# A hybrid mLSTM and attention encoder layer: two output products of the long set turned into seven block products, with their weights prepared in the first stage

## The chip, the cores and the metric

The kernel runs on one core of one Trainium2 chip. The metric is the device time of one execution in microseconds; lower is better. The kernel before takes 2188.54 us, the median of three runs that lie between 2187.59 and 2189.1. One further execution was profiled.

## The reference, cut to what matters

One encoder layer is applied to two sets of tokens with shared weights: a long set (`x_prompt`, 1 x 1024 tokens) and a short set (`x_sample`, 1 x 512 tokens), each token 1024 wide.

```
h    = rms_norm(x, pre_w)
cols = h @ w_in                      # q|k, v, o, z, gates of the mLSTM; q,k,v of the attention; z; two merge gates
y_m  = mlstm_mixer(...) * silu(m_z)                  # (tokens, 1024)
y_a  = dilated_attention(...) * silu(a_z)            # (tokens, 512)
p_m  = y_m @ w_proj_m                                # 1024 x 1024 weights
p_a  = y_a @ w_proj_a                                #  512 x 1024 weights
merged = sigmoid(g_m) * p_m + sigmoid(g_a) * p_a
out  = merged @ w_out                                # 1024 x 1024 weights
y    = x + rms_norm(out, post_w)
```

The change concerns the last five lines for the long set. Everything is float32 in the reference.

## The kernel before, in words

**How a product is made.** TensorE multiplies in a reduced format, so each float32 operand is split into a high part and a low part (`hi` on ScalarE by a copy, `lo = x - hi` on VectorE), and one product of a 128x128 block of weights with 128x512 activations takes three matmuls of 128x512: hi·hi, lo·hi, hi·lo. These three are one *step* (`mm3`, lines 230 to 236). A product over 1024 inputs sums eight steps in one PSUM bank; then VectorE evicts it.

**The stages**, by the time in the profiled execution:

- 0 to 231 us: input norm and value products of the long set.
- 231 to 955 us: 38 "pair iterations" (`unit_pair`). Each loads the weights of two 128-column units (`pw_raw`), lets GpSimd (POOL) form sums of them (`psum_w`), splits raw weights and sums into high and low (`phla`, `phlb`, line 764 is the low part), and does the 1024x1024 product for 1024 tokens as seven block products instead of eight (84 matmuls, 19 us). What follows the products differs: 12 attention iterations, then four times (conv, conv, gate), then 8 "zo" and 2 "az".
- 955 to 1776 us: the mLSTM of the long set, the attention of the long set, and the mLSTM of the short set with the mix of the long set's three attention groups. Between their matmuls TensorE takes *fill*: a list of dense units for the short set (its w_in product and others), one step at a time, taken from a generator (class `Fill`).
- 1776 to 2026 us: attention of the short set ("attention B", 48 rounds), with fill between its small matmuls.
- 2026 to 2096 us: "combine B" mixes the three attention groups of the short set, four 128-token tiles t = 0 to 3: weights of the groups (lines 2033 to 2043), three scaled copies (L2050), two adds (L2056), four transposes on TensorE into `tp` (L2061), a product with the gate (L2063). Fill runs between them.
- 2096 to 2178 us: the rest of the fill, alone.

**The fill of the late stages.** From step 768 on (`SHORT`) the fill is: 32 steps left of the short set's units; for each 512-token half of the long set w_proj_m (64 steps), w_proj_a (32) and w_out (64); the same 160 for the short set; 512 steps in all. `branches` makes w_proj_m and w_proj_a, `final` w_out. Each unit's 512 KB of weights is loaded raw into `wraw` by the POOL queue and split by `split_w` (L296 on ScalarE, L302 on VectorE). `STEPS = (316, 260, 192, 290, 86)` gives the number of steps for five stages: 290 over the 48 rounds of attention B, 86 over combine B. The remaining 136 run alone.

**What sets the order.** Engines run their instructions in program order. That order comes from the generators above: a round or a combine part asks the fill for its share of steps, and the splits, evictions and DMA issues belonging to a step are emitted with it. In the late stages the POOL queue issues the loads (`N.side`), SP the stores.

## Time and profile before

| | |
|---|---|
| median of three runs | 2188.54 us (2187.59 to 2189.1) |
| span of the profiled execution | 2185.1 us |
| last TensorE instruction ends | 2177.8 us |
| busy: TensorE / VectorE / ScalarE / GpSimd | 2173.5 / 1460.8 / 1085.1 / 704.2 us |
| moved by DMA | 395.62 MB, mean 181 GB/s |

The profiled execution's own time is its span, 2185.1 us. A busy time counts the union of the instructions' windows. Matmuls are pipelined and their ends are modelled, so the mean duration of a matmul is longer than the distance from one start to the next; the rate is read from starts. In the rows of the groups the columns are line, engine, operation, output<-inputs, shapes and count, then busy time, mean ns of one, then the engine's idle time before them and what ended it. In the windows, `(x222)` is the number of instructions in the stretch.

### The profile page before, as it was taken

How to read it: one execution, taken by the hardware profiler on the slowest of the kernel's cores; microseconds unless marked ns; L12 is line 12 of the kernel's file. 1: busy time of each engine (PE TensorE's matmuls, PEld its weight loads, DVE VectorE, ACT ScalarE, POOL GpSimd, SP SyncE). 2: the span in 40 equal slices, each digit the busy share in tenths (PEclk: the TensorE clock that was granted, in tenths of full speed). 3: DMA queues.
4: the chain of work that ended last, by engine and by line, in shares of the span. 5: the costliest groups of instructions: out<-in, count | busy, mean ns of one | idle time of the engine just before them, and what ended most of it. 6: DMA issues, size and time to landing. Idle time of an engine off the chain costs nothing.

```text
span 2185.1 us, 33611 instructions
## 1 busy us (share of the span) xinstructions
PE 2173.5 (99%) x11626; PEld 1857.3 (85%) x11626; DVE 1460.8 (67%) x2927; ACT 1085.1 (50%) x2228; POOL 704.2 (32%) x989
## 2 busy tenths in 40 slices
PE   9999999999999999999999999999999999999998
PEld 8988888888888888888888889999788888888887
DVE  8766564657778555547888775574668855656674
ACT  7322333444444343446777656666756544554332
POOL 1000332333333222326776650011045522232331
PEclk9999999999999999999999999999999999999999
DMA  3642454733333222367646558877668786776772
GB/s 139 193 139 73 146 162 144 227 110 116 107 115 114 75 82 97 135 216 261 202 164 225 175 167 262 240 241 196 203 233 278 248 288 205 229 261 187 242 240 106
DMA packets 205748, 395.62 MB, mean 181 GB/s; under 512 B 36393, under 2 KB 117993, under 8 KB 205578
## 3 DMA queue, kind: packets, MB, share of 16 engines
q1 hardware_dynamic: 175272, 281.39, 40.2%
q0 software_dynamic: 26704, 99.50, 13.8%
q10 hardware_dynamic: 3602, 12.59, 1.4%
q8 instruction: 92, 1.51, 0.3%
q14 instruction: 78, 0.64, 0.1%
HBM read 274.71 MB, written 118.69 MB: 180 GB/s over the span
## 4 chain that ended last, share of the span: by engine, by line
PE 97%; DVE 1%; ACT 1%; DMA 1%; issue 0%; POOL 0%; DVEq 0%; POOLq 0%; ACTq 0%
PE d L233 14%; PE d L235 14%; PE d L234 14%; PE dense L233 13%; PE dense L234 13%; PE dense L235 13%; PE lg L1801 2%; PE pt L1831 2%; PE o L1874 1%; PE num L233 1%; PE num L235 1%; PE num L234 1%; PE num L1494 1%; PE o L1853 1%; PE a L1201 1%; PE kv L233 1%
## 5 line engine op out<-in xcount | busy, mean ns | idle before, releaser
L233 PE MATMUL dense<-H,wh 128*128 128x512 f32 x664 | 269.3, 406 | 0.0
L234 PE MATMUL dense<-H,wh 128*128 128x512 f32 x664 | 260.3, 392 | 0.0
L235 PE MATMUL dense<-H,wl 128*128 128x512 f32 x664 | 260.2, 392 | 0.0
L233 PE MATMUL d<-Hh,phla 128*128 128x512 f32 x608 | 236.5, 389 | 0.0
L235 PE MATMUL d<-Hh,phla 128*128 128x512 f32 x608 | 236.5, 389 | 0.0
L234 PE MATMUL d<-Hl,phla 128*128 128x512 f32 x608 | 236.5, 389 | 0.0
L302 DVE TENSOR_TENSOR wl<-wraw,wh 128x1024 fp32r<-128x1024 f32 (+1 forms) x121 | 150.8, 1248 | 57.9 <-ACT wh L296 57.8
L235 PE MATMUL d<-Hh,phlb 128*128 128x512 f32 x456 | 177.4, 389 | 0.0
L233 PE MATMUL d<-Hh,phlb 128*128 128x512 f32 x456 | 177.4, 389 | 0.0
L234 PE MATMUL d<-Hl,phlb 128*128 128x512 f32 x456 | 177.4, 389 | 0.0
L296 ACT ACTIVATE wh<-wraw 128x1024 fp32r<-128x1024 f32 (+1 forms) x124 | 128.1, 1036 | 62.1 <-PE dense L234 24.3
L235 PEld LDWEIGHTS dense<-H,wl 128*128 128x128 f32 x664 | 124.7, 188 | 28.1
L782 POOL TENSOR_TENSOR psum_w<-pw_raw 128x512 f32<-128x512 f32 x38 | 56.7, 1492 | 271.1 <-DMA pw_raw<-w_in 259.9
L1820 DVE CUSTOM_DVE_ANT_0 ls<-lg,bias 128x256 f32<-128x256 f32 (+2 forms) x240 | 78.7, 350 | 90.3 <-PE lg L1801 61.7
L233 PEld LDWEIGHTS dense<-H,wh 128*128 128x128 f32 x664 | 125.0, 188 | 16.4 <-issue 1.2
L234 PEld LDWEIGHTS dense<-H,wh 128*128 128x128 f32 x664 | 125.2, 189 | 14.7
L235 PEld LDWEIGHTS d<-Hh,phla 128*128 128x128 f32 x608 | 114.1, 188 | 23.7
L234 PEld LDWEIGHTS d<-Hl,phla 128*128 128x128 f32 x608 | 114.1, 188 | 23.7
L233 PEld LDWEIGHTS d<-Hh,phla 128*128 128x128 f32 x608 | 114.1, 188 | 23.7
L800 POOL TENSOR_TENSOR psum_w<-pw_raw,psum_w 128x512 f32<-128x512 f32 x38 | 49.3, 1298 | 254.2 <-DVE phla L764 254.2
L1824 ACT ACTIVATE ls<-ls,nm 128x256 f32<-128x256 f32 (+1 forms) x192 | 87.3, 456 | 70.2 <-DVE nm L1822 47.0
L233 PE MATMUL d<-v,Hh 128*128 128x484 f32 (+1 forms) x336 | 121.3, 361 | 0.1
(665 smaller groups left out, 5838.8 us busy)
## 6 DMA issues: line engine op xcount, KB each, us to landing
pw_raw<-w_in SPq DMA_DIRECT2D x76, 512.0 KB, 3.9
wraw<-w_in SPq DMA_DIRECT2D x63, 512.0 KB, 4.4
aqk_a<-pwk SPq DMA_DIRECT2D x32, 512.0 KB, 6.7
wraw<-w_pm POOLq DMA_DIRECT2D x24, 512.0 KB, 5.9
wraw<-w_out POOLq DMA_DIRECT2D x24, 512.0 KB, 3.7
Q<-aqk_a SPq DMA_DIRECT2D x20, 512.0 KB, 6.3
wraw<-w_v POOLq DMA_DIRECT2D x22, 430.0 KB, 6.5
aqk_b<-sw SPq DMA_DIRECT2D x36, 256.0 KB, 7.2
```

The costliest lines, as they stand in the source:

```text
L233: nc.tensor.matmul(out, lh, rh, start=start, stop=False, **kw)
L234: nc.tensor.matmul(out, lh, rl, start=False, stop=False, **kw)
L235: nc.tensor.matmul(out, ll, rh, start=False, stop=stop, **kw)
L296: high = nc.scalar.activation(hi[:, :n], raw[:, :n], AF.Copy)
L302: low = (self.lows or nc.vector).tensor_sub(lo[:, :n], raw[:, :n], hi[:, :n].bitcast(F32))
L782: self.nc.gpsimd.tensor_add(s[:, 0], ws[1][:, 0], ws[1][:, 1])
L800: nc.gpsimd.tensor_sub(s[:, 1], wa[:, 1], s[:, 1])
L1201: nc.tensor.matmul(p[:, c - c0], kT[:, ct, c * P:(c + 1) * P], qT[:, ct, c * P:(c + 1) * P], start=ct == 0, stop=ct == 1)
L1801: nc.tensor.matmul(lg[:, hh], q[hh][:, qs], z.rearrange("p (n j) -> p n j", j=P)[:, pair], start=z is k[hh], stop=z is not k[hh])
L1820: nc.vector.tensor_tensor_reduce(out=ls[rows, hh], in0=ts["lg"][hh][rows, of], in1=bt[rows, hh, by], scale=1.0, scalar=NEG, op0=OP.add, op ...
L1824: self.held = self.held[-3:] + [nc.scalar.activation(ls[:, hh], ls[:, hh], AF.Exp, bias=nm[:, hh:hh + 1], accum_out=ot[:, 128 + hh:129 + hh])]
L1831: nc.tensor.transpose(pp[:, hh * nk + x], ts["ls"][:, hh, x * P:(x + 1) * P], self.ident)
```

## The change

For the long set, w_proj_m and w_out become seven block products over all 1024 tokens at once. Inputs, weights and outputs are cut into 2 x 2 blocks of 512; three of the seven products use a raw quadrant of the weights (0, 1 and 3 in `QUADS`), four a sum of quadrants (4 to 7); the sums of activations are made on VectorE in the late stage (`outputs`: `combined`, `third`, `second`), split there, and multiplied. Per product 16 steps, seven products: 112 steps for w_proj_m and 112 for w_out, where there were 128 and 128. After step 768 the fill has 32 + 112 + 64 + 112 + 160 = 480 steps.

The weights of these products, and w_proj_a, are now split in the first stage. Each of the first 32 pair iterations takes one extra job: 16 `pre_plain` (load 512 KB raw, split it) and then 16 `pre_sums` (load 1 MB, two or four additions on POOL, split), each with a store of 1 MB of high and low parts to a DRAM scratch `pre`. In the late stage `load_pre` loads these parts ready made (1 MB a unit) in place of load and split. The short set's w_proj_m and w_out are still loaded raw and split late; its w_proj_a comes from `pre`.

The long set's input is copied to its output by eight DRAM to DRAM copies early in the program; in the late stage 16 DMAs of the POOL queue add the normalised result onto it (`accum_op`), so its `xo` loads and plain stores are gone. `STEPS` becomes `(316, 260, 192, (6, 5), 16, 50)`: six steps a round for the first 32 rounds of attention B, five for the last 16 (272), then 16 and 50 in combine B; 142 steps remain after it.

```diff
-STEPS = (316, 260, 192, 290, 86)
+STEPS = (316, 260, 192, (6, 5), 16, 50)
+QUADS = (0, 1, 5, 6, 3, 4, 7)
+PRE_A, PRE = 28, 32
...
+    def pre_split(self, x, units, sb, to):
+        nc, n = self.nc, x.shape[1]
+        hl = sb.tile([P, 2, 2, BLK], F32R, name="phlb", bufs=2)
+        nc.scalar.activation(hl[:, 0, :n], x, AF.Copy)
+        nc.vector.tensor_sub(hl[:, 1, :n], x, hl[:, 0, :n].bitcast(F32))
+        for j, u in enumerate(units):
+            y = hl.rearrange("p z a c -> p z (a c)") if to is None else hl[:, :, j]
+            dst = self.pre[u] if to is None else self.pre[u, :, :, to]
+            nc.sync.dma_start(dst.rearrange("z p c -> p z c"), y.bitcast(F32))
...
+    def pre_sums(self, i, sb):
+        nc, q = self.nc, self.a["w_q"]
+        u, c, both = i // 4, slice(i // 2 % 2 * BLK, (i // 2 % 2 + 1) * BLK), i % 2
+        ws = []
+        for b in range(2):
+            w = sb.tile([P, 2, BLK], F32, name="pw_raw", bufs=4)
+            nc.sync.dma_start(w, q[2 * b:2 * b + 2, u, :, c].rearrange("q p c -> p q c"))
+            ws.append(w)
+        wa, wb = ws
+        s = sb.tile([P, 2, BLK], F32, name="psum_w", bufs=2)
+        nc.gpsimd.tensor_add(s[:, 0], wb[:, 0], wb[:, 1])
+        nc.gpsimd.tensor_sub(s[:, 1], s[:, 0], wa[:, 0])
+        if both:
+            nc.gpsimd.tensor_sub(s[:, 1], wa[:, 1], s[:, 1])
+            nc.gpsimd.tensor_sub(s[:, 0], wa[:, 0], wb[:, 0])
+        self.pre_split(s, [4 * QUADS.index(j) + u for j in ((6, 7) if both else (4, 5))], sb, c)
...
+    def load_pre(self, u):
+        hi, lo = self.wsplit.pop(0)
+        self.wsplit.append((hi, lo))
+        for z, x in enumerate((hi, lo)):
+            self.loaded = self.side.dma_start(x[:, :1024].bitcast(F32), self.pre[u, z])
+        return hi[:, :1024], lo[:, :1024]
...
+    def outputs(self, T, before):
...
+        def final(weights):
...
+            def close(b, t, ys):
...
+                for h, y in enumerate(ys):
+                    nc.vector.scalar_tensor_tensor(y, y, s[:, 6:7], pw[:, c], op0=OP.mult, op1=OP.mult)
+                    self.adds.append((n + 5 + 4 * h, lambda y=y, c=c: nc.gpsimd.dma_start(T.y[r0:r0 + P, c], y, accum_op=OP.add)))
...
-            units += N.branches(A, 1, 1, finals[:1]) + N.branches(B, 0, 0, finals[1:2]) + finals[2:]
+            first, final = N.outputs(A, short[-4:])
+            units = short[:-4] + first + N.branches(B, 0, 0, [final]) + [last]
...
+                        if early:
+                            job, *x = early.pop(0)
+                            job(*x, sb)
+                        if kind == "conv":
+                            with tc.issue_after(N.split_end.ins):
+                                t = rows.pop(0)
+                                nc.sync.dma_start(A.y[P * t:P * (t + 1)], A.x[P * t:P * (t + 1)])
```

In combine B the order on TensorE around the first transpose of the mix (`tp`, from the operand `X`) was, before:

```order
L233 MATMUL dense<-Q_17486,H_18682 128x512
L234 MATMUL dense<-Q_17486,H_18682 128x512
L235 MATMUL dense<-Q_17486,H_18683 128x512
L2061 MATMUL tp_20301<-ident,X_20055 128x128 x4
L233 MATMUL dense<-Q_17486,H_18682 128x512
L234 MATMUL dense<-Q_17486,H_18682 128x512
L235 MATMUL dense<-Q_17486,H_18683 128x512
```

and is now (`sw`, `V0b`, `V1b`, `wh_7463` belong to the last block product of the long set's w_out; `H_20408` and `X_20409` are high and low of the short set's y_m):

```order
L235 MATMUL dense<-wh_7463,V1b 128x512
L236 MATMUL dense<-wl_7464,V1b 128x512
L237 MATMUL dense<-wh_7463,V1b 128x512
L235 MATMUL dense<-H_20408,wh_7465 128x512
L236 MATMUL dense<-X_20409,wh_7465 128x512
L237 MATMUL dense<-H_20408,wl_7466 128x512
L2110 MATMUL tp_20629<-ident,X_20364 128x128 x4
L235 MATMUL dense<-H_20408,wh_7465 128x512
L236 MATMUL dense<-X_20409,wh_7465 128x512
```

The first transpose moved from the middle of the long set's last w_out to three matmuls behind its end, in the short set's w_proj_m. Between the four transposes there were 42, 45 and 42 dense matmuls; there are now 33, 30 and 33.

On VectorE the stretch around the product with the first `tp` (L2063 before, L2112 now) was:

```order
L2050 TENSOR_TENSOR Q_20056<-V1a,cw_20231 128x512 x3
L302 TENSOR_TENSOR wl_7153<-wraw_7147,wh_7152 128x1024
L2266 SCALAR_TENSOR_TENSOR ss<-ss 128x1
L2268 TENSOR_TENSOR mg<-dense,postw 128x512
L2056 TENSOR_TENSOR Q_20056<-Q_20056 128x512
L2271 SCALAR_TENSOR_TENSOR xo_17492<-sw_7265,ss,xo_17492 128x512
L2271 SCALAR_TENSOR_TENSOR xo_17493<-mg,ss,xo_17493 128x512
L302 TENSOR_TENSOR wl_7149<-wraw_7146,wh_7148 128x1024
L2063 TENSOR_TENSOR az_20052<-tp_20301,az_20052 128x512
L2056 TENSOR_TENSOR Q_20056<-Q_20056 128x512
```

and is now (L2105 the last add that the first transpose reads, L2446 and L2471 the end of the long set's w_out, L2198 the low parts of the short set's y_m, L304 the low parts of its raw weights):

```order
L2105 TENSOR_TENSOR X_20364<-X_20364 128x512
L2446 SCALAR_TENSOR_TENSOR H_19733<-H_19733,ss,postw 128x512
L2446 SCALAR_TENSOR_TENSOR H_20136<-H_20136,ss,postw 128x512
L2198 TENSOR_TENSOR K_20411<-ymr_17801,H_20410 128x512
L2084 TENSOR_TENSOR cw_20553<-V1a,cw_20553 128x24
L304 TENSOR_TENSOR sw<-wraw_7459,sw 128x1024
L2446 SCALAR_TENSOR_TENSOR H_19733<-H_19733,ss,postw 128x512
L2446 SCALAR_TENSOR_TENSOR H_20136<-H_20136,ss,postw 128x512
L2471 TENSOR_TENSOR H_19733<-H_19733,dense 128x512
L2441 SCALAR_TENSOR_TENSOR ss<-ss 128x1
L2112 TENSOR_TENSOR az_20361<-tp_20629,az_20361 128x512
L304 TENSOR_TENSOR wl_7464<-wraw_7460,wh_7463 128x1024
```

Before, the second add of the second mix stood directly behind the product with the first `tp`; now 24 instructions stand between that product and the add that the second transpose waits for.

In the pair iterations the SP queue held only the pair's loads and the iteration's stores:

```order
L777 DMA pw_raw<-w_in 128x1024 x2
L243 DMA qk_a<-pwk 128x1024 x2
L777 DMA pw_raw<-w_in 128x1024 x4
L243 DMA qk_a<-pwk 128x1024 x2
L777 DMA pw_raw<-w_in 128x1024 x2
```

and now has the job's loads (`w_q`) and stores (`pre`) between the two loads of a pair:

```order
L815 DMA pw_raw<-w_q 128x2x512 x2
L245 DMA qk_a<-pwk 128x1024 x2
L779 DMA pw_raw<-w_in 128x1024
L799 DMA pre<-phlb 128x2x512 x2
L779 DMA pw_raw<-w_in 128x1024
```

The pair's second load now stands behind a store that waits for the job's split on VectorE.

324 lines of the change are left out of this document (301 added, 23 removed).

## The prediction

> **What bounds the kernel now.** I read the totals first, then the chain of waits, TensorE's waits, the windows by stage, and the timeline of one stretch. The page:
>
> ```profile
> span 2185.1 us, 33611 instructions
> PE 2173.5 (99%) x11626; PEld 1857.3 (85%) x11626; DVE 1460.8 (67%) x2927; ACT 1085.1 (50%) x2228; POOL 704.2 (32%) x989
> PEclk9999999999999999999999999999999999999999
> PE 97%; DVE 1%; ACT 1%; DMA 1%; issue 0%; POOL 0%; DVEq 0%; POOLq 0%; ACTq 0%
> ```
>
> TensorE is busy from end to end at a full granted clock, and the chain that ended last is 97% TensorE. Its waits, all four of them:
>
> ```profile
> PE d L2370 <- DMA Hh<-prew: 2.3, 1, 2.3
> PE d L476 <- ACT Hh L470: 0.5, 1, 0.5
> PE d L420 <- DVE u2b L417: 0.5, 1, 0.5
> PE d L235 <- DVE Hl L472: 0.4, 1, 0.4
> ```
>
> Together 3.7 us in the whole run. So a matmul removed comes off the time, and everything else costs nothing until it makes TensorE wait. The question is which engine has little room where the change adds work. Windows (columns: stretch, length, then busy time and instructions of PE, PEld, DVE, ACT, POOL, then clock, DMA share, GB/s):
>
> ```profile
> 400.00:450.00 50.00, 50.00 (x222) 41.42 (x221) 32.45 (x32) 23.68 (x20) 19.16 (x14) 1.00 0.71 211
> 592.90:611.90 19.00, 19.00 (x86) 15.73 (x85) 16.95 (x17) 8.93 (x9) 7.27 (x6) 1.00 0.29 104
> 630.90:650.00 19.10, 19.10 (x86) 15.79 (x85) 11.63 (x13) 6.54 (x7) 7.06 (x9) 1.00 0.36 116
> 1776.00:1800.00 24.00, 24.00 (x132) 20.75 (x131) 14.20 (x37) 14.71 (x34) 6.29 (x12) 1.00 0.90 316
> 1850.00:1900.00 50.00, 50.00 (x278) 43.39 (x278) 34.99 (x90) 26.99 (x72) 14.51 (x27) 1.00 0.72 236
> 2050.00:2096.00 46.00, 45.87 (x209) 37.71 (x208) 39.54 (x83) 12.79 (x22) 19.05 (x33) 1.00 0.85 283
> ```
>
> Two places stand out on VectorE: a conv pair iteration (592.9 to 611.9, 16.95 of 19 us busy) and combine B (39.54 of 46). A gate iteration (630.9 to 650) has room, and so has attention B (1850 to 1900).
>
> **What is removed from TensorE.** Two products of 128 steps become 112 each: 32 steps in all, and by the lists of instructions the matmuls of 128x512 fall by 96. Their price is the distance between starts, not the duration shown:
>
> ```profile
> 2065.20 0.39 PE L234 MATMUL dense<-Q,H 128*128 128x512 f32 x1
> 2065.43 0.39 PE L235 MATMUL dense<-Q,H 128*128 128x512 f32 x1
> 2065.66 0.60 PE L2061 MATMUL tp<-ident,X 128*128 128x128 f32 x4
> 2066.01 0.48 PE L233 MATMUL dense<-Q,H 128*128 128x512 f32 x1
> 2075.67 0.60 PE L2061 MATMUL tp<-ident,Q 128*128 128x128 f32 x4
> ```
>
> 42 dense matmuls and one transpose group (0.35 us from its start to the next) take 2075.67 - 2065.66 = 10.01 us, so 0.23 each; where no transpose lies near, the distance is 0.225 to 0.227 (the first window: 222 in 50 us). 96 x 0.227 = **21.8 us saved**. (By the 0.39 of the rows it would be 37.)
>
> **Combine B.** In both kernels the four transposes need operands that VectorE mixes. Before, they are 42 to 45 dense matmuls apart (10 us); after, 30 to 33 (7.0 to 7.8 us), and the first comes 3 matmuls behind the end of the long set's w_out, on whose results VectorE has just then a pile of work. What VectorE's instructions cost is again the distance from start to start:
>
> ```profile
> 2059.56 0.18 DVE L2039 TENSOR_TENSOR wd<-wd 128x8 f32<-128x8 f32 x1
> 2059.78 0.17 DVE L2040 TENSOR_TENSOR wd<-wd 128x8 f32<-128x8 f32 x1
> 2061.64 1.89 DVE L2050 TENSOR_TENSOR Q<-V1a,cw 128x512 f32<-128x512 f32 x3
> 2063.45 1.22 DVE L302 TENSOR_TENSOR wl<-wraw,wh 128x1024 fp32r<-128x1024 f32 x1
> 2064.58 0.15 DVE L2266 SCALAR_TENSOR_TENSOR ss<-ss 128x1 f32<-128x1 f32 x1
> 2064.65 0.69 DVE L2268 TENSOR_TENSOR mg<-dense,postw 128x512 f32<-128x512 f32 x1
> 2065.25 0.69 DVE L2056 TENSOR_TENSOR Q<-Q 128x512 f32<-128x512 f32 x1
> 2065.85 0.75 DVE L2271 SCALAR_TENSOR_TENSOR xo<-sw,ss,xo 128x512 f32<-128x512 f32 x1
> 2066.51 0.75 DVE L2271 SCALAR_TENSOR_TENSOR xo<-mg,ss,xo 128x512 f32<-128x512 f32 x1
> ```
>
> A split of 128x1024 holds the engine 1.13 us, a 128x512 0.60, with a scalar operand 0.66, a small dependent one about 0.2 (0.07 where independent). The rows' durations run past the next start. The Trainium skill, "Perfetto Trace Analysis", section "Optimizing Scalar/DVE Operations", says that a shown latency counts an overhead about twice because the write acknowledgement overlaps the next instruction; the trace agrees (0.69 shown, 0.60 from start to start). By full durations the sum below would come out some 3 us larger (38 large ones by 0.07 to 0.09).
>
> I anchor at the TensorE matmul that ends the last tile of product 5 of the long set's w_out. From there to the second transpose TensorE has 84 dense matmuls and one transpose group: 84 x 0.227 + 0.35 = 19.4 us. In VectorE's order, from the eviction of that tile to the add that the second transpose reads, stand: 5 splits of the short set's raw w_proj_m (5 x 1.13 = 5.65), 6 evictions (3.6), 8 normalising products (8 x 0.66 = 5.3), 7 splits of y_m rows (4.2), 6 scaled copies and 4 adds of the mixes (6.0), the gate product with the first transpose (0.6), one eviction of the short set (0.66), 24 small ones (4.8). Sum 30.8 us. The difference, **11.4 us, is a wait of TensorE**, most of it at the second transpose. About half is forced even if VectorE were on time at the last eviction of w_out: behind it stand 13.8 us of work, and TensorE has 36 matmuls and a transpose group there, 8.5 us. This gives the lower bound of 5.3; less than that needs VectorE faster than in any row. The upper bound: what VectorE itself waits for comes on top. The rows of ScalarE and DMA that bear on it:
>
> ```profile
> 2073.00 1.22 DVE L302 TENSOR_TENSOR X<-wraw,X 128x1024 fp32r<-128x1024 f32 x1 [1.33 <-ACT X L296]
> ...
> L296 ACT ACTIVATE wh<-wraw 128x1024 fp32r<-128x1024 f32 (+1 forms) x124 | 128.1, 1036 | 62.1 <-PE dense L234 24.3
> wraw<-w_pm POOLq DMA_DIRECT2D x8, 512.0 KB, 6.3
> Q<-az_b POOLq DMA_DIRECT2D x1, 256.0 KB, 8.8
> ```
>
> The fifth raw w_proj_m is loaded when the third split frees its buffer; issue about 0.5, landing 6.3, the high part 1.04 make 7.9 us, and VectorE has 8.4 us of other work up to the split. It fits with 0.5 to spare; a landing of 8.8, the longest row of this stage, would add 2. Waits for ScalarE like the 1.33 us of the first row are possible too. So 5.3 to 17, and I take 11.4, the sum without them. After the second transpose VectorE has 4 to 10 us of work for each 7 us of matmuls, and nothing more is late; the wait costs the stage's end one for one.
>
> **The pair iterations.** Each of the first 32 gets a load, a high part on ScalarE, a low part on VectorE (1.13) and a store; 16 have 2 or 4 additions on POOL. TensorE's order there is unchanged. ScalarE is busy 9 of 19 us and DMA at 0.29 to 0.36: 1.5 to 2 MB more per 19 us is some 80 to 105 GB/s beside 104 to 116, below the 316 seen. That is hidden. The stores stand on SP ahead of a load of the next pair; the load is wanted a third of an iteration later, with the splits due only at the second and fourth product. VectorE's room is the issue, since additions on POOL stretch its two-input work:
>
> ```profile
> 583.58 2.20 DVE L764 TENSOR_TENSOR phla<-pw_raw,phla 128x1024 fp32r<-128x1024 f32 x1
> 584.65 2.28 POOL L785 TENSOR_TENSOR pw_raw<-pw_raw 128x512 f32<-128x512 f32 x1
> L764 DVE TENSOR_TENSOR phla<-psum_w,phla 128x1024 fp32r<-128x1024 f32 x6 | 7.3, 1218 | 0.0
> L782 POOL TENSOR_TENSOR psum_w<-pw_raw 128x512 f32<-128x512 f32 x5 | 6.9, 1382 | 31.8 <-DMA pw_raw<-w_in 31.8
> ```
>
> The same split takes 2.20 beside an addition and 1.22 alone: one addition can cost VectorE 1 us. A conv iteration with a job then needs 16.95 + 1.13 + 2 to 4 = 20.1 to 22.1 us of 19.04, a gate iteration 11.63 + 1.13 + 2 to 4 = 14.8 to 16.8. Two convs (one with 2, one with 4 additions) overrun by 4.1; the gate gives 2.3 to 4.3 back, and the splits have about 5 us of slack (due at the fourth product, three products of 2.7 us into the iteration, less the split). Of four triples the first has mostly plain jobs. So the loss is between 0 and 9.2 (if no gate gave anything back: 1.04 + 1.04 + 3.04 + 3.04 + 1.04); I take 1.0, near the low end, because the triple's sum, 57, just fits 57.1. The Trainium skill, "Perfetto Trace Analysis", same section, says that GpSimd and VectorE share a read port and that moving work from one to the other might not help: the stretched pair of rows agrees, and it speaks against summing here.
>
> **Attention B.** Gone: late splits of the long set's weights. New: 96 more VectorE instructions of 128x512 (58 us) against 12 fewer of 128x1024 (13.6), so 44 us more in 250. VectorE is busy 28 to 35 of 50 us there and would be at 0.75 to 0.88. Single rounds are heavier, and a late high and low part delays one step; attention's own small chains cover it with other steps only in part. 0 to 5 us (one round is 5.2), taken as 0.5. DMA: a unit is 1 MB instead of 512 KB, one for every eight steps, that is for some 7 us at six steps a round of 5.2 us, so 512 KB more make 75 GB/s; on 316 in the densest window that is 391, but there the fill is still the old 32 steps, and on the 236 of the later window it is 311. Hidden, with four units loaded ahead. The x to y copies lie on SP in front of the value stores, in a stretch in which DMA does nothing:
>
> ```profile
> 20.00:50.00 30.00, 29.36 (x203) 27.44 (x202) 29.13 (x41) 22.82 (x46) 1.08 (x1) 1.00 0.00 1
> ```
>
> POOL's new 16 adding DMAs replace 16 loads and 16 stores.
>
> **Sum.** -21.8 + 11.4 + 1.0 + 0.5 = -8.9 us. The span would be 2176.2; the profiled execution stands 3.4 us below the median, so the forecast in runs is 2188.5 - 8.9 = **2179.6 us**.
>
> **Rivals.** (1) *All hidden.* The four PSUM banks and matmuls still in hand let VectorE catch up, no wait at the transposes: -21.8, 2166.7. For it: the present combine B is at 39.54 of 46 busy and TensorE waits 0.13. Against: the order puts both evictions and mixes in one queue. Chance 0.13. (2) *VectorE overruns in the conv iterations and gates don't give back*: 9.2 in place of 1.0, so -0.7, 2187.8; against it the gate's 11.63. With milder forms, 0.21 for a result within 0.2% (4.4 us, about what can be told from no change). (3) *Slower: the fifth w_proj_m weights come late.* Everything up to the second transpose stands behind their split on VectorE, one for one. Landing must exceed 6.3 by 0.5 + 8.9 = 9.4 us, 15.7 us in all, before the gain is gone; the adding DMAs queue ahead of that load on POOL, each of them waiting for a normalising product. At 20 us: +4.3, 2192.8, and each later raw unit then drags too, 2195. Chance with other losses 0.14. (4) That the matmuls don't fall is excluded by the lists of both kernels.
>
> **Numbers.** The main case (a gain of 4.4 to 18) has 0.52, all hidden 0.13, so faster 0.65; same 0.21; slower 0.14. The range runs from all hidden, 2166, to 2191, into rivals 2 and 3 but not to their ends.
>
> **What would show it.** 6490 matmuls of 128x512 on TensorE; a wait of TensorE for VectorE of 8 to 14 us at the line of the transposes (now L2110), split between first and second, with VectorE busy without a gap there; none or 1 to 2 us before 955 us at conv iterations; attention B shorter by some 18 steps. No wait at the transposes, or waits for DMA there, would make the sum wrong; so would a conv iteration longer than 19.04 us three times in a row.

## The result and the profile after

The changed kernel is slower: 2224.62 us, median of four runs (2223.09 to 2226.32), against 2188.82 for the kernel before on the same chip (2187.59 to 2189.78). The ratio is 1.0165, with a 95% interval of 1.0151 to 1.018. The forecast was 2179.6, with a range from 2166 to 2191. The page of the profiled execution, whose span is 2224.6 us (before 2185.1):

```profile
span 2224.6 us, 33846 instructions
...
PE 2171.1 (98%) x11530; PEld 1847.5 (83%) x11530; DVE 1549.0 (70%) x3011; ACT 1084.2 (49%) x2248; POOL 810.4 (36%) x1053
...
PEclk9999999999999999999999999999999999999899
...
DMA packets 233655, 469.05 MB, mean 211 GB/s; under 512 B 38249, under 2 KB 120361, under 8 KB 233354
```

TensorE has 96 instructions fewer, as forecast, but is busy only 2.4 us less; VectorE has 88 us and GpSimd 106 us more work; 73 MB more are moved. TensorE's longest waits, which before were four of together 3.7 us:

```profile
PE d L237 <- DVE phla L766: 12.3, 7, 2.1
PE tp L2110 <- DVE cw L2092: 5.9, 1, 5.9
PE tp L2110 <- DVE X L2105: 5.4, 1, 5.4
PE lg L1847 <- DVE ot L1866: 4.0, 1, 4.0
PE dense L235 <- DVE H L2471: 3.1, 1, 3.1
```

Three places wait: `d` (products of the pair iterations, for the low parts of their weights), `lg` (first logits of attention B) and the transposes `tp` with their surroundings in combine B. Windows that begin and end at the same TensorE instructions show how much each place lost (columns as above: length, then busy time and count of PE, PEld, DVE, ACT, POOL, then clock, DMA share, GB/s). First the kernel before:

```profile
573.80:707.10 133.30, 133.30 (x590) 110.36 (x589) 102.49 (x103) 55.23 (x57) 48.57 (x43) 1.00 0.32 112
...
1772.30:1809.70 37.40, 37.40 (x203) 32.29 (x202) 22.77 (x59) 22.11 (x53) 11.40 (x22) 1.00 0.92 320
1809.70:2018.00 208.30, 208.30 (x1152) 177.09 (x1150) 125.80 (x341) 102.08 (x280) 55.70 (x103) 1.00 0.68 217
2018.00:2177.80 159.80, 159.59 (x726) 130.87 (x721) 101.17 (x188) 53.28 (x100) 46.89 (x85) 1.00 0.60 202
```

and the changed kernel: pair iterations 18 to 24 (counted from 0), the start of attention B, the rest of it, and combine B to the end.

```profile
575.00:729.70 154.70, 141.00 (x589) 112.99 (x588) 127.06 (x114) 60.58 (x66) 85.61 (x65) 0.97 0.57 196
...
1799.20:1844.50 45.30, 40.30 (x204) 33.93 (x203) 20.51 (x60) 17.24 (x47) 8.76 (x17) 0.92 0.86 304
1844.50:2043.80 199.30, 197.73 (x1101) 167.43 (x1099) 130.66 (x370) 82.85 (x264) 52.57 (x100) 1.00 0.77 245
2043.80:2216.00 172.20, 155.54 (x680) 125.72 (x675) 104.84 (x205) 50.27 (x105) 56.89 (x91) 0.96 0.68 206
```

In the first row the same matmuls take 154.7 us instead of 133.3. Of the 21.4 us, 13.7 are idle time (154.70 - 141.00); the other 7.7 are shown as *busy* time, at a mean clock of 0.97. The whole ledger, from starts of the same TensorE instructions in both traces (a matmul less counts 0.227 us):

| stage | before | changed | matmuls fewer | loss |
|---|---|---|---|---|
| up to the first pair product | 231.0 | 232.3 | | 1.3 |
| pair iterations | 723.4 | 744.7 | | 21.3 |
| mLSTM and attention of the long set, mLSTM of the short | 817.9 | 822.2 | | 4.3 |
| attention B, to its 31st `lg` | 37.4 | 45.3 | | 7.9 |
| attention B, the rest | 208.3 | 199.3 | 51: 11.6 | 2.6 |
| combine B to the last TensorE instruction | 159.8 | 172.2 | 45: 10.2 | 22.6 |
| behind it | 7.3 | 8.6 | | 1.3 |
| span | 2185.1 | 2224.6 | 21.8 | 61.3 |

So the 21.8 us are there, and 61.3 us were lost elsewhere: 61.3 - 21.8 = 39.5. How far one trace can be trusted for a stage is seen in the experiments below, where an edit leaves a stage as it is: the pair iterations then take 743.5 to 745.1 us, the start of attention B 44.4 to 46.4, its rest 198.4 to 199.3, combine B 170.8 to 173.7. The first row takes 231.0 to 232.4 and the third 819.2 to 822.8, so their 1.3 and 4.3 us are one trace's figures.

**Clock.** TensorE's timeline behind one wait of the pair iterations:

```profile
580.27 0.39 PE L236 MATMUL d<-Hl,phla 128*128 128x512 f32 x1
582.49 0.50 PE L237 MATMUL d<-Hh,phla 128*128 128x512 f32 x1 [1.82 <-DVE phla L766]
...
583.58 0.63 PE L237 MATMUL d<-Hh,phla 128*128 128x512 f32 x1
584.00 0.63 PE L235 MATMUL d<-Hh,phla 128*128 128x512 f32 x1
...
586.47 0.40 PE L235 MATMUL d<-Hh,phla 128*128 128x512 f32 x1
```

Behind a wait of 1.82 us the matmuls start 0.42 to 0.43 us apart for some 3 us, then 0.23 again: seven of them, 1.4 us on top of the wait. Of six waits of 1.8 to 2.1 us in this stage three had such a tail and three had none. In all, 22 matmuls of the row start 0.41 to 0.43 us apart, which makes 4.4 of the 7.7 us. The other 3.3 are not in such tails: the first distance behind a wait is 0.34 us, and idle time is counted only from the modelled end of the matmul ahead, 0.39 us behind its start, so that each wait is shown some 0.16 us too short. The Trainium skill, "TensorE: Matmul & The Clock Gate", Part 1, describes a clock that falls to half behind an idle window of about 3.4 us and gives 426.7 ns from start to start at half rate for this width, with windows that run free of the kernel. The 0.427 us and the length of the tail agree; that waits of about 2 us are enough, some of the time, is what this trace adds.

**VectorE in a conv iteration with a sum job** (the timeline of the changed kernel ahead of the first late product):

```profile
561.64 1.94 DVE L766 TENSOR_TENSOR phlb<-pw_raw,phlb 128x1024 fp32r<-128x1024 f32 x1
563.51 4.55 DVE L878 SCALAR_TENSOR_TENSOR pwk<-c,cws,pwk 128x1024 f32<-128x1024 f32 x2
567.98 1.78 DVE L766 TENSOR_TENSOR phlb<-psum_w,phlb 128x512 fp32r<-128x512 f32 x1
...
575.29 2.29 DVE L766 TENSOR_TENSOR phla<-pw_raw,phla 128x1024 fp32r<-128x1024 f32 x1
```

and GpSimd in the same microseconds, with the job's additions:

```profile
562.58 2.15 POOL L820 TENSOR_TENSOR psum_w<-psum_w,pw_raw 128x512 f32<-128x512 f32 x1
...
566.94 2.27 POOL L823 TENSOR_TENSOR psum_w<-pw_raw 128x512 f32<-128x512 f32 x1
```

A split of 128x1024 takes 1.94 us beside the job's additions instead of 1.22, and 2.29 beside the pair's own additions that follow them. The last row (`phla`) ends at 577.58, and the matmul that reads it starts at 577.63. From 554.8 to 585.4 VectorE has no idle time of more than 0.11 us. How much room was used up is seen at the low part for the second product of iteration 18. In the kernel before, it is ready 3.77 us early:

```profile
572.00 1.22 DVE L764 TENSOR_TENSOR phla<-psum_w,phla 128x1024 fp32r<-128x1024 f32 x1
...
576.99 0.39 PE L235 MATMUL d<-Hh,phla 128*128 128x512 f32 x1
```

Over iterations 14 to 25 this lead is 3.8 to 6.0 us before. In the changed kernel it is 2.3 us in iteration 15, 1.0 in iteration 17 and gone (0.05) in 18, 20, 21, 23 and 24. At 19, 22 and 25 it is 1.0 to 2.0 us again, and that is about what TensorE itself was slowed by half rate just before (some 1.75).

**Combine B.** VectorE's timeline around the last eviction of product 5 (first row: its wait for the groups' sums; then the first and the last instruction of the pile that the prediction summed):

```profile
2079.14 0.17 DVE L2082 TENSOR_TENSOR cw<-V0a 128x8 f32<-128x8 f32 x1 [9.26 <-DMA V0a<-og_b]
...
2081.37 0.68 DVE L2470 TENSOR_TENSOR H<-H,dense 128x512 f32<-128x512 f32 x1
...
2110.19 0.69 DVE L2105 TENSOR_TENSOR Q<-Q 128x512 f32<-128x512 f32 x1
```

From 2081.37 to 2110.88 it is 29.5 us, with 0.91 us idle in it; the prediction's sum was 30.8. TensorE's two waits at the transposes are 5.9 and 5.4, together 11.3 us, as forecast (8 to 14). But the 9.26 us ahead of VectorE's pile were not in the prediction, nor TensorE's wait of 3.1 us for an eviction that stands on VectorE behind that wait. The DMA issues of that stretch (size, median us to landing), in the kernel before

```profile
V0a<-og_b SPq DMA_DIRECT2D x1, 792.0 KB, 4.0
...
og_b<-sg SPq DMA_DIRECT2D x2, 132.0 KB, 2.4
```

and in the changed one:

```profile
V0a<-og_b SPq DMA_DIRECT2D x1, 792.0 KB, 7.1
...
y_prompt<-K POOLq DMA_DIRECT2D x3, 256.0 KB, 8.8
...
og_b<-sg SPq DMA_DIRECT2D x2, 132.0 KB, 10.0
```

The store of the last attention sums took 10 us instead of 2.4. The load of the mix reads what it wrote, so SP stood until it landed, and the load was itself slower.

### The profile page after: what moved, and what is told of

Its sections match the earlier page's. It is cut to its first block, busy times and chain, and to the rows that moved or that the text cites. A ratio compares the mean times of both kernels' runs of the same rounds, so it can differ in the third digit from the quotient of the medians.

```text
span 2224.6 us, 33846 instructions
## 1 busy us (share of the span) xinstructions
PE 2171.1 (98%) x11530; PEld 1847.5 (83%) x11530; DVE 1549.0 (70%) x3011; ACT 1084.2 (49%) x2248; POOL 810.4 (36%) x1053
## 4 chain that ended last, share of the span: by engine, by line
PE 59%; DVE 6%; DMA 4%; issue 4%; ACT 1%; POOL 1%; SPq 0%; DVEq 0%; POOLq 0%; ACTq 0%
PE dense L235 11%; PE dense L236 11%; PE dense L237 11%; PE d L237 4%; PE d L235 4%; PE d L236 4%; PE lg L1847 2%; DVE pwk L878 2%; PE pt L1877 2%; PE o L1920 1%; PE num L235 1%; PE num L236 1%; PE num L237 1%; DVE phla L766 1%; PE num L1540 1%
## 5 line engine op out<-in xcount | busy, mean ns | idle before, releaser
L237 PE MATMUL dense<-H,wl 128*128 128x512 f32 x688 | 271.4, 395 | 0.0
L237 PE MATMUL d<-Hh,phla 128*128 128x512 f32 x608 | 239.4, 394 | 12.3 <-DVE phla L766 12.3
L235 PE MATMUL d<-Hh,phla 128*128 128x512 f32 x608 | 238.5, 392 | 1.4 <-ACT phla L765 1.4
L237 PEld LDWEIGHTS dense<-H,wl 128*128 128x128 f32 x688 | 130.3, 189 | 29.3
L304 DVE TENSOR_TENSOR wl<-wraw,wh 128x1024 fp32r<-128x1024 f32 (+1 forms) x96 | 120.8, 1260 | 29.7 <-ACT wh L298 29.7
L298 ACT ACTIVATE wh<-wraw 128x1024 fp32r<-128x1024 f32 (+1 forms) x99 | 101.7, 1030 | 47.8 <-PE dense L236 20.0
L237 PE MATMUL d<-v,Hl 128*128 128x484 f32 (+1 forms) x336 | 120.6, 359 | 0.4 <-DVE Hl L474 0.4
```

Source lines behind the costliest of these rows:

```text
L235: nc.tensor.matmul(out, lh, rh, start=start, stop=False, **kw)
L237: nc.tensor.matmul(out, ll, rh, start=False, stop=stop, **kw)
L298: high = nc.scalar.activation(hi[:, :n], raw[:, :n], AF.Copy)
L304: low = (self.lows or nc.vector).tensor_sub(lo[:, :n], raw[:, :n], hi[:, :n].bitcast(F32))
```

## Experiments on the pair iterations

Each edit is against the changed kernel; "stage" is the time from the first to the last product of the pair iterations, 723.4 us before and 744.7 in the changed kernel. The letters of the theories change between the expectations: the store of a job, which holds a `phlb` buffer that the pair needs, is rival B in the first run and theory C in the later ones, where B is the second raw tile.

**Additions left out.**

```diff
-        nc.gpsimd.tensor_add(s[:, 0], wb[:, 0], wb[:, 1])
-        ... (all of the job's additions)
+        s = wa
```

> The 16 sum jobs of the pair iterations split the raw quadrants as loaded; their 2 or 4 additions on GpSimd are left out (so four of the seven weight blocks hold other values). Loads, splits and stores stay. Measured before this run: the pair iterations cost 21.4 us more than in the kernel before, 13.7 of them waits of TensorE, the rest matmuls at a lower clock behind the waits. Theory A, VectorE is overrun because the additions on GpSimd stretch its two-input work: a conv iteration then needs some 18.2 of 19.04 us, the waits go to 0 to 2 us, the stage loses 3 us or less, and the time is about 2204. Rival B, the job's store holds the phlb buffer that the pair's own split needs (ScalarE waits 36 us for such stores between 540 and 760 us): the loss stays at 15 us or more, the time at 2218 to 2224.

2219.8 us (2215.28 to 2220.73), ratio 1.0138 [1.0123, 1.0153]; stage 741.6. Still 18.2 of the 21.3 us are lost, in iterations 18, 21, 23 and 24 (the changed kernel loses in 20 too), though the additions are gone from GpSimd; this is what rival B had forecast. So the additions are not a necessary cause.

**One raw tile instead of two, additions kept.**

```diff
-        wa, wb = ws
+            break                # after the first load
+        wa = wb = ws[0]
```

> A sum job loads one raw tile (512 KB) in place of two and adds the halves of that tile; number and size of additions, low parts and stores stay as they are. The values of the sums are wrong. Theory A (additions and VectorE's room): the pair stage still loses 17 to 21 us, 2220 to 2225. Theory B (the second raw tile): the loss falls to 0 to 5 us, 2203 to 2209. Theory C (stores): still 17 to 21.

2224.86 us (2223.63 to 2225.38), ratio 1.0164 [1.0149, 1.0179]; stage 743.8. Nothing gained: the second load is not a necessary cause either.

**Both left out** (both edits above).

> A sum job loads one raw tile and splits it without any addition: sum jobs become plain jobs in load, split and store (32 alike; values of the sums wrong). With both loads and no additions the pair stage lost some 17 us. Theory B: the loss falls to 0 to 3 us, 2203 to 2207. Theory C: it stays at 14 to 17 us, 2216 to 2221. Theory A holds that the additions were half of it and VectorE's room the rest: 3 to 10 us, 2206 to 2214.

2209.47 us (2208.96 to 2209.85), ratio 1.0094 [1.0079, 1.0109]; stage 730.0, loss 6.6. TensorE's wait for `phla` in the kernel with additions and one tile:

```profile
PE d L237 <- DVE phla L766: 12.1, 10, 2.1
```

and in this one, with a wait of ScalarE beside it:

```profile
PE d L237 <- DVE phla L766: 1.8, 5, 0.5
```

```profile
ACT phlb L765 <- DMA pre<-phlb: 97.8, 30, 7.0
```

So *either* part of a sum job, additions or second raw tile, is enough to lose 18 to 20 us, and a job with neither loses 6.6. ScalarE's total wait for stores to free `phlb` does not tell these kernels apart: it is 97.8 us here, where little was lost, and 90.8 in the changed kernel. Which product of TensorE waits does tell them apart. In the changed kernel and in the one with one tile it is always the first or second product of an iteration, for `phla`, at the end of VectorE's work (or of ScalarE's behind it). In the kernel without additions more than half of the wait is at the last product, for `phlb`:

```profile
PE d L235 <- ACT phlb L765: 5.8, 4, 2.5
PE d L237 <- DVE phla L766: 5.5, 6, 1.4
PE d L237 <- DVE phlb L766: 1.2, 3, 0.5
```

There the high part that ScalarE makes for this product starts at 595.02, 658.34 and 722.46 us in iterations 18, 21 and 24, each time 0.10 or 0.11 us behind the landing of a job's store (594.92, 658.23 and 722.36): the store holds the buffer. It was issued 10.0 to 11.8 us into these iterations; with one tile and no additions it was issued at 6.6 to 8.2, and the product gets its operand with hardly a wait. So two chains are seen, each enough alone: VectorE's work where there are additions, a job's late store where there are two tiles and no additions.

**Jobs in other iterations, same work.** In the changed kernel the sum jobs begin in iteration 16 and the loss in iteration 18; the three conv iterations with plain jobs (12, 13, 15) took 19.04 us, like all attention ones. So the list was re-ordered: plain jobs into the eight convs, sums into four attention iterations, the gates and zo.

```diff
+                    plain, added = early[:16], early[16:]
+                    early = plain[:8] + added[:4]
+                    for i in range(4):
+                        early += plain[8 + 2 * i:10 + 2 * i] + [added[4 + i]]
+                    early += added[8:]
```

> Only the list of jobs is re-ordered: the 16 plain jobs now lie in the first 8 attention iterations and in the 8 conv iterations, the 16 sum jobs in the last 4 attention iterations, the 4 gate and the 8 zo ones. Same work in total. In the changed kernel the pair stage loses 21.4 us, all of it in iterations 18 to 24 (convs and their gates with sum jobs). Theory A (VectorE and GpSimd together have no room in a conv iteration for a sum job: additions, their stretching of VectorE and the low part): the loss goes to 0 to 4 us, the kernel takes 2203 to 2209. Theory B (a sum job takes two of the four raw-weight buffers and delays the pair's own weights, whatever the iteration): the loss moves to the attention and zo iterations, 10 to 20 us remain, 2214 to 2224. Theory C (the store of a job holds a buffer of high and low parts, plain jobs too): the convs still lose, 2218 to 2224.

2207.9 us (2206.55 to 2210.5), ratio 1.0089 [1.0074, 1.0104]; stage 730.3, loss 6.9. No work was taken away and 14.4 of 21.3 us are gone; the attention, gate and zo iterations carry the sum jobs in 19.04 us each, but for 2.2 us in the first zo. The wait for `phla` is 4.7 us (six times). Theory B (the second raw tile, wherever it stands) is out, and C (the stores) as the main cause of the 21.3. Theory A's forecast, a loss of 0 to 4 us, is missed by 3: iterations 18 and 21, convs that now hold plain jobs, and the first zo still lose 2.5, 1.9 and 2.2 us.

**No job in the last four convs.** The freed jobs stand in az and two of the last gate iterations.

```diff
+                    early = plain[:14] + added[:1] + plain[14:] + added[1:2] + [None] * 2 + added[2:3] + [None] * 2 + added[3:]
```

> The 32 jobs are placed anew: plain ones in the 12 attention iterations and in the first four convs (which lost nothing with plain jobs), sums in the gates, zo, az and two of the last gate iterations, none in the last four convs. Pair stage: with plain jobs in all convs 6.9 us were left of 21.4. If a job costs only where it stands, the loss falls to 0 to 2 us and the kernel to 2201 to 2204. If jobs in the gate between two convs are enough to delay the following conv, 4 to 7 us remain, 2205 to 2209.

2205.18 us (2204.61 to 2206.77), ratio 1.0075 [1.006, 1.009]; stage 726.2, loss 2.8, in three iterations around convs and gates. By the difference, plain jobs in those convs cost some 4 us as well. A coarser form of it:

**No job in any conv**: a sum job in each attention and gate iteration, and a plain one more in every second attention iteration and in zo and az.

> The same 32 jobs, but none in a conv iteration: the sums in the 12 attention and 4 gate iterations, the plain ones in zo and az iterations and every second attention iteration. Theory A (VectorE has no room in conv iterations): TensorE's waits in the pair iterations vanish, the stage loses 0 to 3 us instead of 21.4, time about 2204. Rival B (the store holding phlb) would also be relieved here, so A and B are told apart by the run without additions. Rival C (the loads and stores themselves, on SP and DMA, wherever they stand): loss stays above 10 us, time above 2213.

2239.61 us (2238.58 to 2240.37), ratio 1.0232 [1.0217, 1.0248]; stage 760.8. The convs ran in 19.0 to 19.2 us, but eight of the ten attention iterations from the third on took 19.8 to 27.8. In these runs an attention iteration holds one job without loss (as in the re-ordered list), and not one and a half on the mean.

**Other buffers.** Two kernels gave the pair's fourth sum a tile of its own, so that a job's store holds less of what the pair needs; the second also leaves the additions out. To make room for it another tile, `pu2`, has one buffer instead of two, so each run changes two things.

```diff
-        us = [sb.tile([P, BLK], F32, name=f"pu{i}", bufs=4 - i) for i in (2, 3)]
-        bs = [sb.tile([P, 2, 2, BLK], F32R, name="phlb", bufs=2) for _ in range(2)]
+        us = [sb.tile([P, BLK], F32, name=f"pu{i}", bufs=1) for i in (2, 3)]
+        bs = [sb.tile([P, 2, 2 - i, BLK], F32R, name=("phlb", "ps4")[i], bufs=2 - i) for i in range(2)]
```

> The jobs get a phlb buffer that the pairs' splits do not use: the pair's last small split (s4) moves into a tile of its own of half the size, so that the two phlb buffers serve one pair split and one job in turn; to fit, the tile pu has one buffer instead of two. Nothing is left out. Theory B, the job's store (5.3 us to land, behind 1 to 2 us of issue) holds the buffer that the pair's next split needs, so ScalarE and VectorE stand still in order: ScalarE's wait for that store, 36 us between 540 and 760, vanishes, the pair iterations lose 0 to 5 us instead of 21.4, time 2203 to 2208. Theory A, VectorE overrun by the stretched work alone: the wait for the store vanishes too, but TensorE's 12 to 14 us of waits stay, time 2219 or more.

> As the run with the own buffer, and the sum jobs' additions on GpSimd left out (four of the seven weight blocks then hold other values). Theory B: no more than 3 us below the run with the own buffer alone, because nothing is left to gain. Theory A with B (each takes part): the own buffer alone keeps 8 us or more, and this run falls to a loss of 0 to 2 in the pair iterations, time 2202 to 2205.

2230.1 us, ratio 1.0191 [1.0174, 1.0208], and 2268.32 us, 1.0363 [1.0348, 1.0379]: both worse. ScalarE's waits in the first say why these tell nothing on the theories:

```profile
ACT ps L765 <- POOL psum_w L846: 94.0, 22, 8.8
...
ACT phlb L765 <- DMA pre<-phlb: 63.5, 16, 7.9
```

The first row is new and the longest: it is the split of the fourth sum into its own tile, at which ScalarE now stands until GpSimd has made that sum. Whether the own tile gave anything behind it, and what the smaller `pu2` cost, can't be read from these two runs.

## Experiments on attention B

**Block sums later.** First by their place in the code:

```diff
-            for f in (third, second):
-                ...
-            jobs = combined("m", ring, uses)
+            jobs = [(0, lambda f=f, k=k: f(k)) for f in (third, second) for k in range(4)] + combined("m", ring, uses)
```

> The eight block sums of the long set's y_m (third and second) are taken out of the 32 steps before w_proj_m and given as the first jobs of w_proj_m, some 12 steps or 10 us later; nothing is left out. Measured: at the start of attention B VectorE waits 9.4 us for a row of y_m at the head of its queue with the softmax behind it, and TensorE loses some 8 us. Theory F, head of line blocking on VectorE: the row has landed by the later time, the loss falls to 0 to 3, time about 2218. Rival G, DMA at 400 GB/s holds up attention's own loads: the loss stays above 6, time 2223 or more.

2223.31 us, ratio 1.0157 [1.014, 1.0174]. VectorE's order stayed exactly as it was, so the run says nothing. Then by a data dependency, so that the sums stand 46 to 64 instructions later on VectorE:

```diff
+                nc.vector.scalar_tensor_tensor(M["a1"][:, k], M["b1"][:, k], zero, M["a1"][:, k], op0=OP.add, op1=OP.subtract)
```

(`zero` is a scalar that ScalarE writes after product 0.)

> The run that gave the block sums later left VectorE's order as it was, since the order there follows data, not the place in the code. Here the first sum takes a zero as scalar operand that ScalarE writes after the fourth tile of product 0, so the eight sums now stand 52 rows later on VectorE, behind the first softmax rounds of attention B. Nothing is left out. Theory F, head of line blocking on VectorE (it waits 9.4 us there for a row of y_m with the softmax behind): the 4.0 us wait of TensorE for ot and most of the 8 us lost at the start of attention B go, time 2217 to 2219. Rival G, DMA at 400 GB/s holds up attention's own loads: VectorE waits for bias or Q instead, loss above 5, time 2221 or more.

2223.2 us (2221.3 to 2225.2), ratio 1.0159 [1.0144, 1.0174]; start of the stage 43.6 us instead of 45.3. VectorE's first softmax now waited for this alone:

```profile
DVE ls L1866 <- DMA bias<-erow: 13.2, 1, 13.2
```

So the block sums ahead of the softmax were not the cause by themselves; the bias was late. Two things make it so. The change flushes the gate stores of `sw` ahead of attention B, since `sw` becomes a weight buffer; SP then stands on two of them, whose units are only being computed, with the bias loads behind. SP's queue, before and changed:

```profile
1766.10 0.94 SPq L274 DMA_DIRECT2D bias<-erow  x2
```

```profile
1795.28 5.04 SPq L251 DMA_DIRECT2D gt_b<-sw  x2
1800.41 0.88 SPq L276 DMA_DIRECT2D bias<-erow  x2
```

The first logits start at 1772.3 before and at 1799.2 after: the bias was issued 6.2 us ahead of them, and is now issued 1.2 us behind. And it lands later, 9.5 us after issue instead of 5.7, in a DMA that moves 396 GB/s from 1795 to 1813 (340 at the same place before); 14 rows of y_m, 256 KB each, are loaded for the new block products from 1780 to 1800.

**Four edits, one a stage or two** (jobs re-ordered as above; sums later; the flush behind the first bias loads; 24 steps ahead of the first transposes):

```diff
             self.need(("table", 0))
+            if T.n <= 4:
+                self.hook()          # flush of N.sw and its new use, moved here
```

(Shown is the moved flush; the order of the jobs and the late sums are the edits above.)

> Four changes in three stages, read stage by stage: jobs re-ordered as in the kernel with sum jobs in gate and zo iterations; at the start of attention B the first bias loads are issued ahead of the two gate stores that the change flushes there, and the block sums for w_proj_m stand later on VectorE; in combine B 24 steps instead of 16 before the first transposes. Theory G (late bias loads on SP and a DMA near 400 GB/s): issuing them ahead of the stores takes 3 to 6 us of the 7.8 lost there. Theory F (the softmax stands behind the block sums on VectorE): moving the sums alone gave nothing at 2223.2, so nothing more here. Combine B: the room takes 5 to 9 us. If the pair stage also gives its 17 to 21 us: 2190 to 2200.

2204.28 us (2203.26 to 2204.55), ratio 1.0069 [1.0052, 1.0086]. The start of attention B took 40.4 us (5 of 7.9 us recovered); with the same two edits in the three later kernels it took 37.6, 37.6 and 39.2, at best all but 0.2. By the difference to the late sums alone, which gave 1.7, most of this is the flush; the flush alone was not run. A part is lost again behind it: in every kernel with the late sums and the same steps a round, the rest of attention B takes 200.8 to 201.9 us instead of 199.3. Combine B gained nothing from 24 steps (172.8).

## Experiments on combine B

"Stage" is here the time from the last `lg` to the last TensorE instruction: 159.8 us before, 172.2 in the changed kernel, 149.6 if only the matmuls counted.

**More steps ahead of the first transposes:**

```diff
-STEPS = (316, 260, 192, (6, 5), 16, 50)
+STEPS = (316, 260, 192, (6, 5), 30, 50)
```

> STEPS[4] from 16 to 30: 14 more steps (42 matmuls, 9.5 us) between the end of attention B and the first transposes of combine B, taken from the bare steps at the end. Theory D, the transposes wait because VectorE has 29.5 us of work between the last tile of product 5 and the second transpose's operand while TensorE has 19.4: with 9.5 us more the two waits (5.9 and 5.4 us) fall to 0 to 2 together, with the lower clock behind them 12 to 16 us are gone, time 2209 to 2213; the wait of 3.1 us for an eviction stays. Rival E, the cause is VectorE's 9.3 us wait for the mix's first load (V0a) at the head of its queue, which comes later too: then the 3.1 us wait goes as well, and all of the 22 us, time 2203. Rival H, the transposes only move and meet the next pile (the short set's weights): waits stay, time 2220 or more.

2215.58 us (2212.51 to 2217.76), ratio 1.0122 [1.0107, 1.0137]; stage 164.5. The waits at `tp` are gone, others came:

```profile
PE dense L236 <- DVE K L2198: 4.3, 1, 4.3
PE dense L235 <- DVE H L2471: 4.0, 1, 4.0
```

The first is for the split of a y_m row of the short set (L2198), the second for an eviction that stands on VectorE behind another such split, which itself waited 8.4 us. The loads of these rows stand on SP behind the load of the mix. The time lies between what theory D (here VectorE's work) and rival H had forecast.

**Half of the adding DMAs left out** (block product 4's eight, 2 MB; that half of the output stays the input):

```diff
-                    self.adds.append((n + 5 + 4 * h, ...
+                    b and self.adds.append((n + 5 + 4 * h, ...
```

> The eight adding DMAs of the long set's first half (block product 4 of w_out, 256 KB each) are left out, so 2 MB less are moved beside the mix's store and load in combine B; that half of the output stays the input. In the changed kernel the store of the last attention sums lands after 11.1 us and the load of the mix behind it after 7.1 (before: 2.4 and 4.0), and VectorE idles 9.3 us for it. Theory D (transfers crowd each other there): the store lands in 3 to 7 us, VectorE's wait for the load falls to 2 to 6 us, TensorE's waits at the first two transposes from 11.3 to 4 to 8 us, 2217 to 2221. Theory V (VectorE's own work of 30 us sets the transposes): the transfers are early, the waits of TensorE stay at 10 to 12 us, 2223 to 2225.

2213.23 us (2212.16 to 2216.22), ratio 1.0115 [1.0098, 1.0132]; stage 162.9, so 9.3 us less. The store of the last attention sums, the load behind it, VectorE's wait for that, and TensorE's only wait left at the transposes:

```profile
V0a<-og_b SPq DMA_DIRECT2D x1, 792.0 KB, 4.0
...
og_b<-sg SPq DMA_DIRECT2D x2, 132.0 KB, 6.1
```

```profile
DVE cw L2082 <- DMA V0a<-og_b: 2.5, 1, 2.5
```

```profile
PE tp L2110 <- DVE cw L2083: 10.5, 1, 10.5
```

(From this run on theory D is the crowd of transfers, and V is VectorE's work.) Theory D holds for what is ahead of the pile: VectorE's wait falls from 9.3 to 2.5. Theory V holds for the pile itself: with the transfers nearly in time, the wait at the transposes is 10.5 us, where the prediction had 11.4. The gain is more than either said. A reservation: the DMAs left out also read tiles (places H1 and K1) that the y_m rows of the short set take over, and some of VectorE's rows moved, so a part of the 9.3 us can be those tiles coming free and not the crowd.

**Mix loaded later, and 30 steps:**

```diff
-                next(mixed)
                 fill.stage(STEPS[4], 4)
                 fill(2)
                 next(mixed)
                 fill(2)
+                next(mixed)
```

> In combine B the load of the first mix is issued after the first eight or more steps of fill instead of ahead of them, so that loads of y_m rows no longer stand behind it on SP, and 30 steps instead of 16 lie ahead of the first transposes. With 30 steps alone the time was 2215.6 and VectorE waited 8.4 us for late y_m rows (TensorE 8.3 there). Theory D: rows land in time, the stage gives another 4 to 8 us, 2208 to 2212. Theory V: the work is the bound, the wait moves back to the transposes, 2214 to 2218.

2214.64 us (2212.11 to 2216.2), ratio 1.0116 [1.0101, 1.0131]; stage 163.0, 1.5 less than with 30 steps alone, which is within the spread of this stage. Theory D's further 4 to 8 us did not come: the store still lands after 9.5 us.

## The cures together

**Three at a time**: own tile, late sums, 24 steps and six a round.

> Own buffer, late sums, and STEPS (316, 260, 192, (6, 6), 24, 50): 24 steps more ahead of the first transpose of combine B than in the changed kernel. If the three places are independent, the gains add: about -18 (pair iterations), -6 (attention B), -13 to -20 (combine B), so 2180 to 2188. If the places share a cause (DMA near its ceiling, a clock that stays low), the sum is short: above 2195.

2231.54 us, ratio 1.0198 [1.0183, 1.0213]. The own tile's loss in the pair iterations (stage 750.6) covers the rest.

**All that had worked**: no job in the last four convs, flush behind the bias loads, late sums, mix later with 30 steps.

> The cures together: jobs out of the four convs, bias loads of attention B ahead of the flushed gate stores, block sums later on VectorE, first mix loaded later and 30 steps of room. If the causes are independent, the gains add: 21 in the pair iterations, 5 at the start of attention B, 12 to 16 in combine B, from 2224.6 to 2183 to 2190, that is within 0.3% of the kernel before. If they only move waits on (as with 24 steps in combine B, which gave nothing), 2193 to 2203.

2192.5 us (2190.39 to 2195.84, ten runs), ratio 1.0018 [1.0008, 1.0027], a little above what independent gains would give. So 32 of the 36 us are recovered with all of the change's work still in the kernel. By its trace the stages lose, in the order of the ledger, 1.1, 2.8, 1.6, 0.2, 4.0, 14.1 and 1.6 us, 25.4 against 21.8 of matmuls. The start of attention B and combine B in it:

```profile
1777.80:1815.40 37.60, 37.60 (x204) 32.33 (x203) 13.55 (x48) 17.10 (x47) 8.62 (x17) 1.00 1.00 370
2016.10:2179.80 163.70, 154.36 (x681) 124.65 (x677) 105.75 (x205) 50.96 (x106) 56.78 (x91) 0.98 0.71 217
```

The DMA is as full as ever in the first row (370 GB/s), without a wait of TensorE. The bias takes even longer to land than in the changed kernel (11.4 us), but it is issued at 1771.6, again 6.2 us ahead of the first logits: the lateness of the issue was what hurt.

**Half of the adding DMAs left out of it:**

> The cures of the kernel at 2192.5, and the eight adding DMAs of the long set's first half left out (that half of the output stays the input). Theory D (adding DMAs crowd combine B and hold its buffers): the stage gives 6 to 10 us, 2182 to 2187, faster than before. Theory V (VectorE's work): 0 to 3 us, 2189 to 2193.

2188.25 us (2185.63 to 2189.7), ratio 1.0 [0.9991, 1.0009]; combine B 159.4, 4.3 us less than with them. Between the two theories. TensorE's largest wait is again the second transpose:

```profile
PE tp L2112 <- DVE X L2107: 7.4, 1, 7.4
```

**Copies later and 40 steps.** The eight input-to-output copies are issued in the long set's mLSTM stage.

```diff
+                N.pending += [(N.clock + 6 + 4 * t, "copy", (A.y[P * t:P * (t + 1)], A.x[P * t:P * (t + 1)]), (N.sg,)) for t in rows]
```

> On top of the cures: the eight input-to-output copies are issued one by one in the long set's mLSTM stage instead of ahead of the first loads, and 40 steps instead of 30 lie ahead of the first transposes. Copies: the first pair iteration starts at 231 us instead of 232.1 (1 us). Room: if VectorE's work in combine B is what is left, 3 to 6 of the 14 us lost there go, 2185 to 2189, level with the kernel before or a little faster. If late transfers are, the wait only changes place, 2189 to 2193.

2198.95 us (2196.7 to 2199.62), ratio 1.0048 [1.0034, 1.0061]. The first pair product starts at 232.4 us, so the copies were not what delayed it (another kernel with the copies in their old place had 231.3, and the 1.3 us are within the spread of that stretch). Combine B took 167.5, 3.8 more than with 30 steps, and the stages ahead of it together some 5 us more, for which no cause was isolated. No version beat the kernel before.

## Why the prediction was wrong, point by point

- **Matmuls, -21.8: right.** 96 fewer, and where nothing waits the rate is 0.227 us.
- **Combine B, 11.4: measured 22.6.** The sum of VectorE's work was right (29.5 us of 30.8), and so was the wait at the transposes (11.3, and 10.5 where half of the adding DMAs are out of the way). Two terms were missing. The upper bound spoke only of the raw weights' loads; what came late was the mix's load behind a store (9.3 us of VectorE's time ahead of the pile). And idle time was priced at its own length: the stage's 172.2 us hold 16.7 idle and 5.9 more of busy time (155.54 against 149.6), of which 16 matmuls at half rate make 3.2.
- **Pair iterations, 1.0: measured 21.3**, over the upper bound of 9.2. The failed step is "the splits have about 5 us of slack" and the gate that "gives 2.3 to 4.3 back". VectorE's extra work was sized about right (127.06 us of busy time against 102.49 in iterations 18 to 24, 3.5 each; the step said 3.1 to 5.1). The slack was there, 3.8 to 6.0 us, though not for the reason given: the low parts that came late are due in the first and second product, not in the fourth. But it was counted as if each triple began with all of it. It is spent once, from iteration 14 to 18, and in the light iterations (18, 21 and 24), which have a job too, no more than TensorE's own half rate gives comes back, where the step counted on 2.3 to 4.3. From then on each low part that VectorE reaches late stops TensorE. The same jobs cost 6.9 with the sums moved to gates, zo and attention. The second term is the store: "That is hidden" looked at the loads behind it on SP, and not at the `phlb` buffer that it holds, which is what the run without additions waits for. And 4.4 of the 21.3 us are matmuls at half rate behind the waits, which the prediction did not price.
- **DMA "hidden" in attention B, and not priced in combine B: wrong in both.** The prediction compared rates (391 and 311 GB/s beside the 316 seen); what counted was, in attention B, when the bias was issued (1.2 us behind the first logits instead of 6.2 ahead of them), and in combine B, when a 132 KB store landed between large transfers (10 us instead of 2.4).
- **Attention B, 0.5: measured 10.5**, of which 7.9 at its start. The flush of `sw` was in the change and its queue was not followed: SP's order put the bias behind two stores that wait. The remaining 2.6, and what the stages between lose (1.3 to 4.9 over all traces), were not priced and no run here isolates them.
- **POOL's adding DMAs, "replace 16 loads and 16 stores", priced at nothing: wrong.** Without half of them combine B is 4 us shorter in the kernel with the cures and 9 in the changed one, with the reservation above.
- **Rivals.** The first (all hidden) did not come: the waits at the transposes are there. The second (convs overrun, gates don't give back) had the right place, with 9.2 of the 21.3 us. The third (raw weights late) did not come: TensorE's waits hold none for raw w_proj_m. Each rival named one cause, while several stages lost at once. Of the observations that were to show the forecast wrong, one was seen, a wait for DMA at the mix (VectorE's 9.26 us). Conv iterations over 19.04 us were seen too, but singly (18 and 21), not three in a row.

What stays open: why the two chains of the pair iterations do not add (about 18 and 20 us alone, 21 together, 6.6 with neither), and what makes the 6.6. Each of these kernels also got another order on VectorE and ScalarE. In combine B it is not told apart how much of the gain without half of the adding DMAs is the crowd and how much the tiles that come free.

## What to carry to other kernels

Room on an engine must be looked for up to each due time, not summed over a loop: place extra work in the iterations whose own operands are not due soon, which here recovered 14 of 21 us without taking any work away. Where a job shares buffers with the loop, follow each buffer until its store has landed. A wait of TensorE can cost more than its length: here three of six waits of about 2 us had 1.4 to 1.6 us of half-speed matmuls behind them. Where a change adds a flush, a store or a 1 MB load, follow the small transfers that stand behind it on the queue or beside it; here the mean rate did not tell when a 132 KB store lands.

## What the runs showed of the hardware

- A wait of 1.8 to 2.1 us was followed in three of six cases by some 3 us of matmuls 0.43 us apart instead of 0.227.
- A 128x512 split on VectorE took 1.78 us beside an addition of GpSimd that took 2.27; the same split took 0.68 at 576.20 us of the kernel before, and a group of five such additions there had a mean of 1.38.
- A 132 KB store between 256 KB adding DMAs and 512 KB loads landed after 10 us instead of 2.4, in a stretch with a mean of only 272 GB/s (1767 packets in 14 us), in which the DMA engines were busy all the same (share 1.04).
